# One conv channel tile handed to ScalarE and adding transfers during the attention, and the sum after the convolution placed later, in a two-layer decoder trunk

## The chip, the cores and the metric

The kernel runs on one core of one Trainium2 chip. The metric is the device time of one execution in microseconds. Every other time is from a hardware profile of one execution, measured from the start of its span.

## The reference

It is a trunk of two layers over 512 tokens with 16 learned meta tokens ahead of them (528 positions), 1024 channels, all in float32:

```python
for i in range(2):
    if i == 0: h = h + fox_conformer_mixer(rms_norm(h), ...)      # the change lies here
    else:      h = h + multiscale_pool_mixer(rms_norm(h), ...)
    h = h + conv_glu_ffn(rms_norm(h), ...)                        # 2 x 2816 channels up, 2816 down
return rms_norm(h)[:, 16:]

def fox_conformer_mixer(h, ...):
    q, k, v, f_logit, glu = split(h @ w_in)                       # 3 x 512, 8, 2 x 512 columns
    attn = forgetting_attention(q, k, v, log_sigmoid(f_logit + b_f))   # 8 heads of 64, causal
    a, g = split(glu)
    u = causal_depthwise_conv(a * sigmoid(g), conv_w, conv_b)     # 512 channels, 31 taps
    u = silu(layer_norm(u, ln_g, ln_b))
    return concat([attn, u]) @ w_out
```

## The kernel before, in words

Activations lie transposed: channels on the 128 partitions, the 528 positions along the free axis. The 512 conv channels are four tiles of 128x528. Products run in split float32: an operand becomes a high part (`...H`) and the rest (`...L`), and a product is three matmuls, in two halves of 264 columns. Weights come in chunks of eight 128x128 tiles: SyncE loads `raw` (512 KB), ScalarE writes `wH` and the negated `wL` (L172, L177), and a transfer of POOL's queue adds `raw` onto `wL` (L178). Three buffers of each hold the chunks.

The even mixer takes about the first 265 us. First come the tiles `a` and `g` of the gated input (`GLU_ORDER`); then the attention, whose order on TensorE is written out by hand in the string `PE_ORDER`. `F` is half of a q, k or v tile (24 matmuls), `O` half of an output tile, and a name with a digit is a step of the attention for the head pair of that digit, A and B being its two heads: `MA` (row maxima of the scores; matmuls into `m`, L664 reduces them into `N`, and L666 to L668 make the pair `E` from that), `EA` (transposes `E` into `e`, which goes into `q2`), `SA` (scores `s`; ScalarE exponentiates them twice, L719 and L721, and VectorE takes the low part `PL`, L722), `V` (transposes v; `VH`, `VL`), `A0` and `A1` (scores times values into `o`). `SUM`, `MEAN`, `VAR` and `SILU` are the layer norm of the convolution.

The convolution runs on VectorE meanwhile. As soon as a gated tile `u[i]` is there, its 31 taps go into the list `queue`. `fill(pace)` is called after each unit of the input products and takes the next `pace` taps off the list. Tap 0 of a tile is a scaled copy with bias on ScalarE (L498); each of the other 30 is one multiply-add on VectorE in place (L500). `PACE` holds the pace by stage: 1.8 while the GLU products run, 2.8 in the first part of the attention, then 5.8. `ln_sum` (`SUM`) empties the list, frees the buffers of `u` and of the even head pairs, adds up the four conv tiles (L762, L772) and loads the residual `hm`; `ln_mean` (`MEAN`) is the matmul `mu` over that sum and what follows it.

Only TensorE's order is fixed by hand there (`manual_schedule`). The queues of the others are ordered by a planner before the run: it goes through the instructions in the order in which they were issued and puts into an engine's queue what its own timeline says is ready, so a tap can stand ahead of work issued before it. At run time each engine works off its queue in order. `after(late, early)` is an edge for the planner alone, without a wait. `COPIES` says for each head pair which engine makes the five kinds of rounded copies of q, k and v (A is ScalarE, V is VectorE).

Of the kernel before, what the change touches and what calls it, by code (L numbers as in the profile page):

```python
# [7 lines left out]
F32 = mybir.dt.float32  # L8
F32R = mybir.dt.float32r
BF16 = mybir.dt.bfloat16  # L10
AF = mybir.ActivationFunctionType
ALU = mybir.AluOpType
# [3 lines left out]
P = 128  # L16
T = 528
# [44 lines left out]
PE_ORDER = ("F F F F F F MA0 F MB0 F EA0 F SA0 V0 EB0 F A10 SB0 / "  # L62
# [3 lines left out]


OUTER = (0, 4)
# [15 lines left out]
POOL_ORDER = ("Z0 S0 D0 Z1 X0 S1 D1 Z2 S2 T2 D2 Z3 S3 Q0 X1 T3 D3 Z4 S4 Q1 X2 T4 D4 Z5 S5 Q2 X3 T5 D5 "  # L84
              "Z6 S6 Q3 X4 T6 D6 Z7 S7 Q4 X5 T7 D7 Q5 X6 X7 Q6 Q7")

PACE = (1.8, 2.8, 5.8, 5.8, 5.8, 5.8)

APART = (2,0,1,0)
SPLIT_FIRST = True  # L90
SQ_AFTER = (None, 0, None, None, 4, None, 6, 7)
NORM_AT = 1

COPIES = ('AAAAA', 'VAAAV', 'AAAAA', 'AAVAV')

FIRST_CHUNKS = 3

# [26 lines left out]
def trunk_kernel(  # L124
# [7 lines left out]
    nc = tc.nc  # L132
# [5 lines left out]
    wk = ctx.enter_context(tc.tile_pool(name="wk", bufs=2))  # L138
# [11 lines left out]
    state = {"pos": 0, "emitted": 0}  # L150
# [6 lines left out]
    def col(c, rows=slice(0, P)):  # L157
        return pt[rows, c:c + 1]
# [52 lines left out]
    cell = {}  # L211
# [14 lines left out]
    def after(late, early):  # L226

        tc.add_manual_dep(late.ins, early.ins.name,
                          mybir.DependencyInfo(mybir.DependencyClass.NoSync, mybir.DependencyReason.DATA),
                          reason="order")  # L230
# [75 lines left out]
    with ExitStack() as mx:  # L306
        mp = mx.enter_context(tc.tile_pool(name="mix", bufs=1))
# [46 lines left out]


        cv = h[0:4]
        scr = h[4:8]
        cH = [mp.tile([P, T], F32R, tag=f"cH{i}", name=f"cH{i}") for i in range(NCONV)]
        aH = [mp.tile([P, T], F32R, tag=f"aH{i}", name=f"aH{i}") for i in range(4)]
# [61 lines left out]
        H8 = slice(0, HEADS)  # L421
# [51 lines left out]
        def done_g(i):  # L473
            t_ = wk.tile([P, T], F32, tag="sq", name=f"sg{i}", bufs=3)

            def fn(hf, ps):
                nc.vector.tensor_tensor(t_[:, half(hf)], ps, cell["R"][:, half(hf)], op=ALU.mult)
                i_ = nc.scalar.activation(t_[:, half(hf)], t_[:, half(hf)], AF.Sigmoid)
                after(i_, state["lastexp"])
                if i == NCONV - 1 and hf == 1:  # L480
                    state["set"] = use_log_exp(i_)
                if hf == 1:
                    uu = u[i][:, CW - 1:]
                    nc.vector.tensor_tensor(uu, uu, t_, op=ALU.mult)
                    for j in range(CW):
                        queue.append((i, j))
            return fn

        def cw(i, j):
            return col(C_CW + i * CW + j)  # L490

        queue = []
        credit = [0]

        def tap(i, j):
            src = u[i][:, j:j + T]
            if j == 0:
                nc.scalar.activation(cv[i], src, AF.Identity, scale=cw(i, j), bias=col(C_CB + i))  # L498
            else:
                nc.vector.scalar_tensor_tensor(cv[i], src, cw(i, j), cv[i], op0=ALU.mult, op1=ALU.add)  # L500

        def fill(pace):
            credit[0] = min(credit[0] + pace, len(queue))
            while credit[0] >= 1:
                tap(*queue.pop(0))
                credit[0] -= 1


        def first_products():

            cell["f"] = wk.tile([P, T], F32, tag="tapp", name="f")[H8, :]
            low = wk.tile([P, T], F32, tag="tapp", name="flow")[H8, :]
            pss = [sp(f"zf{hf}")[0:40, :TH] for hf in range(2)]
            a0 = [pp(f"ps_a0_{hf}")[:, :TH] for hf in range(2)]
            ws = [next_weight(("in", "a", 0, k)) for k in range(KT)]
            sums = [sp(f"ssq{x}")[:, :TH] for x in range(2)]
            for k in range(KT):
                sq = first_square(k)
                for x in (xH, xL):
                    for hf in range(2):  # L520
                        mm(pss[hf], wfs[:, k, :], x[k][:, half(hf)], k == 0 and x is xH, k == KT - 1 and x is xL)
                    for hf in range(2):
                        mm(a0[hf], ws[k][0], x[k][:, half(hf)], k == 0 and x is xH, False)
                square_sums(sums, 0, [sq], k == 0, k == KT - 1)
            for hf in range(2):
                for k in range(KT):
                    mm(a0[hf], ws[k][1], xH[k][:, half(hf)], False, k == KT - 1)
                pending.append((done_a(0), hf, a0[hf]))
            for hf, ps in enumerate(pss):
                nc.scalar.copy(cell["f"][:, half(hf)], ps[H8, :])  # L530
                nc.scalar.copy(low[:, half(hf)], ps[32:40, :])
            nc.vector.tensor_tensor(cell["f"], cell["f"], low, op=ALU.add)
            return sums
# [71 lines left out]
        def attention(p):  # L605
# [25 lines left out]
            def maxima(hh):  # L631
                tl = st[hh]
                N = tl["N"]
                for x, parts in enumerate((((2, 0, 272), (1, 0, 144), (0, 0, 16)), ((3, 0, 400),),
                                           ((4, 0, TH),), ((4, TH, T),))):
                    s_ = sp(f"m{p}_{hh}_{x}")
# [28 lines left out]
                E = tl["E"]  # L665
                nc.vector.tensor_tensor(N[:, 4:5], N[:, 4:5], N[:, 5:6], op=ALU.min)  # L666
                nc.vector.tensor_copy(E[:, :, 0], N[:, 0:5])
                nc.vector.tensor_tensor(E[:, :, 1], N[:, 0:5], E[:, :, 0].bitcast(F32), op=ALU.subtract)  # L668

            def rows(hh):  # L670
                tl = st[hh]
# [88 lines left out]
        def sum_of(x, y, name):  # L760
            t_ = wk.tile([P, T], F32, tag="sq", name=name, bufs=3)
            nc.vector.tensor_tensor(t_, x, y, op=ALU.add)  # L762
            return t_

        def ln_sum():
            fill(len(queue))
            early.close()
            lp = mx.enter_context(tc.tile_pool(name="late", bufs=1))
            cL.extend(lp.tile([P, T], F32R, tag=f"cL{i}", name=f"cL{i}") for i in range(NCONV))
            hm.extend(lp.tile([P, T], F32, tag=f"hm{m}", name=f"hm{m}") for m in range(KT))  # L770
            a1, a2 = sum_of(cv[0], cv[1], "mu0"), sum_of(cv[2], cv[3], "mu1")
            nc.vector.tensor_tensor(a1, a1, a2, op=ALU.add)  # L772
            cell["mu"] = a1
            for m in range(KT):
                nc.sync.dma_start(hm[m], hT[:, m, :])

        def ln_mean():
            pss = channel_mean(cell["mu"], "mu")
            for i in range(NCONV):
                for hf in range(2):  # L780
                    nc.vector.scalar_tensor_tensor(cv[i][:, half(hf)], pss[hf], -1.0 / (P * NCONV),
                                                   cv[i][:, half(hf)], op0=ALU.mult, op1=ALU.add)
            for i in range(NCONV):
                s_ = wk.tile([P, T], F32, tag="tapp", name=f"csq{i}")
                nc.scalar.activation(s_, cv[i], AF.Square)
                if i == 0:
                    first = s_
                elif i == 1:
                    cell["var"] = sum_of(first, s_, "var")
                else:  # L790
                    nc.vector.tensor_tensor(cell["var"], cell["var"], s_, op=ALU.add)
# [410 lines left out]
```

## Time and profile before

| | |
|---|---|
| time, median of 3 runs | 1074.52 us (1073.5 to 1074.99) |
| the profiled execution | 1075.98 us, of which the span is 1074.2 us |
| TensorE, matmul | 96% of the span busy |
| ScalarE | 58% |
| VectorE | 51% |
| GpSimd (POOL) | 17% |
| granted TensorE clock, mean | 0.981 of 2.4 GHz |

Busy shares are means over stages that differ much. The views below give, for a stretch, the busy time of each engine (with the number of instructions), the granted clock and the mean share of the 16 DMA engines; for a wait, who waited for whom; and for a DMA, how long it took from its issue to its landing.

### The profile page before, as it was taken

To read this page: it belongs to the slowest core of one execution; us is meant where nothing else is said; L and a number is where in the kernel's file an instruction comes from. 1 tells how busy PE (TensorE), PEld (TensorE's weight loads), DVE (VectorE), ACT (ScalarE), POOL (GpSimd) and SP (SyncE) were. 2 spreads that over 40 slices of the span, in tenths; PEclk is the share of its full clock that TensorE was granted. 3 is DMA by queue.
4 is the path that set the end of the run, shared out by engine and by line. 5 is a ranking of instruction groups with operands and counts; after the bars stand their busy time and mean duration, and the time that the engine had idled before them with its cause. 6 is when DMAs were issued, how large, how long until landed. Compare 5 with 4: busy or idle time off the path is not lost.

```text
span 1074.2 us, 20092 instructions
## 1 busy us (share of the span) xinstructions
PE 1033.4 (96%) x8376; PEld 1021.7 (95%) x8376; DVE 548.9 (51%) x917; ACT 623.7 (58%) x876; POOL 181.4 (17%) x302
## 2 busy tenths in 40 slices
PE   9996879999999999999999998799999999999996
PEld 8996879999999999999999998699999999999995
DVE  5799996876048641035444225608742125445214
ACT  7662647786467653345556557457764345565542
POOL 5210111001111111111111112311111111111111
PEclk9998889999999999999999999799999999999998
DMA  6774223637978778778777777977888788787852
GB/s 218 170 189 114 55 65 85 194 77 173 254 165 181 180 178 200 166 182 180 176 187 179 175 186 169 196 175 181 179 195 191 168 189 178 187 189 185 190 117 79
DMA packets 53291, 179.85 MB, mean 167 GB/s; under 512 B 6352, under 2 KB 8400, under 8 KB 53200
## 3 DMA queue, kind: packets, MB, share of 16 engines
q0 software_dynamic: 25136, 86.65, 44.7%
q1 hardware_dynamic: 26720, 90.68, 25.8%
q8 instruction: 66, 1.08, 0.4%
q10 hardware_dynamic: 1344, 1.23, 0.4%
q14 instruction: 25, 0.20, 0.1%
HBM read 89.80 MB, written 2.10 MB: 86 GB/s over the span
## 4 chain that ended last, share of the span: by engine, by line
PE 82%; DVE 12%; ACT 2%; issue 2%; DMA 1%; POOL 0%; DVEq 0%; POOLq 0%; ACTq 0%
PE up L197 47%; PE dn L197 23%; DVE h L500 7%; PE wo L197 3%; PE ps_v L197 1%; DMA h<-ws 1%; PE ps_k L197 1%; PE ps_q L197 1%; PE pl L197 1%; PE s L197 1%; PE o L197 1%; PE ssq L197 1%; PE m L197 1%; DVE N L664 1%; DVE PL L722 0%
## 5 line engine op out<-in xcount | busy, mean ns | idle before, releaser
L172 ACT CAST wH<-raw 128x1024 fp32r<-128x1024 f32 x162 | 170.0, 1049 | 252.3 <-PE up L197 122.0
L197 PE MATMUL up<-xH,wH 128*128 128x264 f32 (+1 forms) x1408 | 287.3, 286 | 8.1 <-ACT xH L261 8.0
L197 PE MATMUL up<-xL,wH 128*128 128x264 f32 (+1 forms) x1408 | 287.5, 286 | 1.2 <-DVE xL L262 1.2
L197 PE MATMUL up<-xH,wL 128*128 128x264 f32 (+1 forms) x1408 | 286.9, 285 | 0.0
L178 POOL DMA_DIRECT2D wL<-raw x159 | 136.9, 861 | 796.7 <-ACT wL L177 744.8
L197 PEld LDWEIGHTS up<-xH,wH 128*128 128x128 f32 x1408 | 220.5, 190 | 9.3 <-ACT xH L261 9.3
L197 PEld LDWEIGHTS up<-xL,wH 128*128 128x128 f32 x1408 | 220.0, 190 | 2.6 <-DVE xL L262 2.6
L197 PEld LDWEIGHTS up<-xH,wL 128*128 128x128 f32 x1408 | 219.5, 190 | 0.0
L177 ACT ACTIVATE wL<-wH 128x1024 fp32r<-128x1024 f32 x159 | 167.3, 1052 | 1.9
L928 DVE SCALAR_TENSOR_TENSOR t<-u,par,t 128x528 f32<-128x528 f32 (+1 forms) x176 | 131.0, 759 | 57.9 <-ACT t L925 54.8
L197 PE MATMUL dn<-gH,wH 128*128 128x264 f32 (+1 forms) x704 | 145.5, 282 | 0.0
L197 PE MATMUL dn<-gH,wL 128*128 128x264 f32 (+1 forms) x704 | 145.2, 282 | 0.0
L197 PE MATMUL dn<-gL,wH 128*128 128x264 f32 (+1 forms) x704 | 145.2, 281 | 0.0
L197 PEld LDWEIGHTS dn<-gH,wH 128*128 128x128 f32 x704 | 110.2, 188 | 0.1
L197 PEld LDWEIGHTS dn<-gL,wH 128*128 128x128 f32 x704 | 110.0, 188 | 0.1
L197 PEld LDWEIGHTS dn<-gH,wL 128*128 128x128 f32 x704 | 109.7, 188 | 0.0
L979 DVE TENSOR_TENSOR h<-dn,h 128x528 f32<-128x528 f32 (+1 forms) x30 | 21.0, 700 | 173.5 <-PE dn L197 173.5
L958 DVE TENSOR_TENSOR u<-up,R 128x528 f32<-128x528 f32 (+1 forms) x74 | 51.7, 701 | 103.9 <-PE up L197 103.6
L500 DVE SCALAR_TENSOR_TENSOR h<-u,par,h 128x528 f32<-128x528 f32 x120 | 86.1, 755 | 0.3
L925 ACT ACTIVATE t<-u,par 128x528 f32<-128x528 f32 (+1 forms) x88 | 71.0, 820 | 0.0
L214 ACT CAST gH<-t 128x528 fp32r<-128x528 f32 (+1 forms) x44 | 27.5, 624 | 44.2 <-DVE t L939 44.0
L215 DVE TENSOR_TENSOR gL<-t,gH 128x528 fp32r<-128x528 f32 (+1 forms) x44 | 30.8, 700 | 25.8 <-ACT gH L214 25.6
(246 smaller groups left out, 1423.5 us busy)
## 6 DMA issues: line engine op xcount, KB each, us to landing
raw<-wts SPq DMA_DIRECT2D x162, 512.0 KB, 4.5
wL<-raw POOLq DMA_DIRECT2D x159, 512.0 KB, 6.2
h<-hT SPq DMA_DIRECT2D x8, 264.0 KB, 5.4
hm<-hT SPq DMA_DIRECT2D x8, 264.0 KB, 4.9
acc<-sq POOLq DMA_DIRECT2D x7, 264.0 KB, 3.3
h<-ws POOLq DMA_DIRECT2D x5, 264.0 KB, 7.6
outT<-y ACTq DMA_DIRECT2D x1, 512.0 KB, 3.1
outT<-y SPq DMA_DIRECT2D x1, 512.0 KB, 3.9
```

Source lines behind the costliest of these rows:

```text
L172: nc.scalar.copy(wH, raw)
L177: nc.scalar.mul(wL, wH.bitcast(F32), -1.0)
L178: nc.gpsimd.dma_start(wL, raw, accum_op=ALU.add)
L197: nc.tensor.matmul(out, lhsT, rhs, start=start, stop=stop)
L214: nc.scalar.copy(oH, src)
L215: nc.vector.tensor_tensor(oL, src, oH.bitcast(F32), op=ALU.subtract)
L500: nc.vector.scalar_tensor_tensor(cv[i], src, cw(i, j), cv[i], op0=ALU.mult, op1=ALU.add)
L664: nc.vector.tensor_reduce(n_, so, axis=AX.X, op=ALU.max, negate=True)
L925: nc.scalar.activation(t_, uu[:, off + 2:off + 2 + nt], AF.Identity, scale=col(c0 + 2), bias=col(c0 + 3))
L928: nc.vector.scalar_tensor_tensor(t_, uu[:, off + x:off + x + nt], col(c0 + x), t_, op0=ALU.mult, op1=ALU.add)
L958: nc.vector.tensor_tensor(v2(ud), ps[:, :, :nu], v2(R[:, tu:tu + 2 * nu]), op=ALU.mult)
L979: nc.vector.tensor_tensor(v2(h[m][:, td:]), ps[:, :, :nd], v2(h[m][:, td:]), op=ALU.add)
```

## The change

- `ADDED = 3`: the taps of conv tile 3 go into a list of their own with its own pace. Tap 0 stays. Tap 1 is a scaled copy on ScalarE into a new tile `cv2`. Each of taps 2 to 30 is a scaled copy on ScalarE into one of three `tapp` buffers, and a transfer of POOL's queue that adds the buffer onto `cv[3]` (even taps) or `cv2` (odd taps).
- `PACE` is a pair for each stage: VectorE's taps 1.8, 2.2, then 3.2; the new list's 0, 0, then 2.1.
- A tap on VectorE gets an edge for the planner behind the last `E` (L668) issued before it, once there is one.
- `SUM` stands behind the last `F`, seven places later in `PE_ORDER`; `MEAN` comes one `EA3` and one `O` later, and `VAR` one `O` later.
- `ln_sum` adds `cv2` onto `cv[3]` on VectorE first.
- All rounded copies go to ScalarE. `tapp` has three buffers in place of two.

```diff
-            "/ V2 F EA2 F SA2 EB2 F A02 SUM A12 SB2 F B02 MA3 B12 F MEAN EA3 O O MB3 O SA3 O V3 VAR O EB3 O SB3 A03 A13 O SILU O O O O O B03 B13 O O O O")
+            "/ V2 F EA2 F SA2 EB2 F A02 A12 SB2 F B02 MA3 B12 F SUM EA3 O MEAN O MB3 O SA3 O V3 O VAR EB3 O SB3 A03 A13 O SILU O O O O O B03 B13 O O O O")
-PACE = (1.8, 2.8, 5.8, 5.8, 5.8, 5.8)
+ADDED = 3
+PACE = ((1.8, 0.0), (2.2, 0.0), (3.2, 2.1), (3.2, 2.1), (3.2, 2.1), (3.2, 2.1))
-COPIES = ('AAAAA', 'VAAAV', 'AAAAA', 'AAVAV')
+COPIES = ('AAAAA', 'AAAAA', 'AAAAA', 'AAAAA')
+        cv2 = mp.tile([P, T], F32, tag="cv2", name="cv2")
-                        queue.append((i, j))
+                        queue[int(i == ADDED)].append((i, j))
-        queue = []
-        credit = [0]
-        def tap(i, j):
+        queue = {0: [], 1: []}
+        credit = [0, 0]
+        def tap(i, j, kind):
             src = u[i][:, j:j + T]
             if j == 0:
                 nc.scalar.activation(cv[i], src, AF.Identity, scale=cw(i, j), bias=col(C_CB + i))
+            elif kind == 1 and j == 1:
+                nc.scalar.activation(cv2, src, AF.Copy, scale=cw(i, j))
+            elif kind == 0:
+                i_ = nc.vector.scalar_tensor_tensor(cv[i], src, cw(i, j), cv[i], op0=ALU.mult, op1=ALU.add)
+                if "rows" in state:
+                    after(i_, state["rows"])
             else:
-                nc.vector.scalar_tensor_tensor(cv[i], src, cw(i, j), cv[i], op0=ALU.mult, op1=ALU.add)
+                pr = wk.tile([P, T], F32, tag="tapp", name=f"tap{i}_{j}", bufs=3)
+                nc.scalar.activation(pr, src, AF.Copy, scale=cw(i, j))
+                nc.gpsimd.dma_start((cv[i], cv2)[j % 2], pr, accum_op=ALU.add)
         def fill(pace):
-            credit[0] = min(credit[0] + pace, len(queue))
-            while credit[0] >= 1:
-                tap(*queue.pop(0))
-                credit[0] -= 1
+            for kind in range(2):
+                credit[kind] = min(credit[kind] + pace[kind], len(queue[kind]))
+                while credit[kind] >= 1:
+                    tap(*queue[kind].pop(0), kind)
+                    credit[kind] -= 1
-                nc.vector.tensor_tensor(E[:, :, 1], N[:, 0:5], E[:, :, 0].bitcast(F32), op=ALU.subtract)
+                state["rows"] = nc.vector.tensor_tensor(E[:, :, 1], N[:, 0:5], E[:, :, 0].bitcast(F32), op=ALU.subtract)
         def ln_sum():
-            fill(len(queue))
+            fill((len(queue[0]), len(queue[1])))
+            nc.vector.tensor_tensor(cv[ADDED], cv[ADDED], cv2, op=ALU.add)
```

## Rows read from the trace of the kernel before

**Rows 1.** The chain that ended last, by engine, over the whole span.

```profile
PE 82%; DVE 12%; ACT 2%; issue 2%; DMA 1%; POOL 0%; DVEq 0%; POOLq 0%; ACTq 0%
```

**Rows 2.** Busy time by stage; the last three numbers: clock, DMA share, GB/s.

```profile
40.00:83.00 43.00, 41.82 (x345) 41.44 (x343) 42.87 (x72) 26.98 (x35) 9.95 (x15) 1.00 0.79 183
83.00:161.00 78.00, 60.63 (x446) 57.54 (x447) 77.12 (x154) 35.19 (x78) 9.21 (x15) 0.87 0.31 75
161.00:204.00 43.00, 43.00 (x362) 41.59 (x360) 28.60 (x73) 31.11 (x73) 4.70 (x7) 1.00 0.54 145
```

**Rows 3.** Waits of TensorE, 81 to 162 us: sum, times, longest.

```profile
PE e L197 <- DVE E L668: 8.2, 1, 8.2
PE e L197 <- DVE N L666: 5.6, 1, 5.6
PE o L197 <- DVE PL L722: 2.8, 2, 1.6
PE m L197 <- DVE k L590: 0.9, 1, 0.9
PE o L197 <- DVE VL L622: 0.6, 1, 0.6
```

**Rows 4.** Timeline of VectorE around two makings of E: start, busy time.

```profile
92.87 0.14 DVE L666 TENSOR_TENSOR N<-N 128x1 f32<-128x1 f32 x1
...
94.10 2.78 DVE L500 SCALAR_TENSOR_TENSOR h<-u,par,h 128x528 f32<-128x528 f32 x4
...
100.92 0.17 DVE L668 TENSOR_TENSOR E<-N,E 128x5 fp32r<-128x5 f32 x1
...
170.74 0.16 DVE L666 TENSOR_TENSOR N<-N 128x1 f32<-128x1 f32 x1
170.94 0.17 DVE L667 CAST E<-N 128x5 fp32r<-128x5 f32 x1
171.14 0.17 DVE L668 TENSOR_TENSOR E<-N,E 128x5 fp32r<-128x5 f32 x1
```

**Rows 5.** Busy time by stretch, of ps_q, ps_k and s alone (TensorE first).

```profile
143.00:150.00 7.00, 5.51 (x24) 5.38 (x24) 0.43 (x1) 0.56 0.01 2
170.00:174.00 4.00, 3.16 (x24) 2.99 (x24) 0.33 (x1) 1.00 0.60 115
...
101.00:107.00 6.00, 4.54 (x24) 4.43 (x24) 0.00 (x0) 0.68 0.20 79
...
118.00:122.00 4.00, 3.43 (x17) 3.16 (x14) 1.79 (x6) 0.52 0.53 162
183.00:186.00 3.00, 1.95 (x17) 1.81 (x14) 0.44 (x2) 1.00 0.00 0
```

**Rows 6.** Busy time by stretch, of the taps on VectorE (L500) alone.

```profile
40.00:83.00 43.00, 34.80 (x50) 1.00 0.79 183
83.00:161.00 78.00, 50.48 (x70) 0.87 0.31 75
```

**Rows 7.** Timelines of VectorE, and the chain that ended last, near the sum.

```profile
67.61 0.69 DVE L484 TENSOR_TENSOR u<-u,sg 128x528 f32<-128x528 f32 x1
...
136.81 0.70 DVE L762 TENSOR_TENSOR mu<-h,h 128x528 f32<-128x528 f32 x1
...
162.64 0.69 DVE L772 TENSOR_TENSOR mu<-mu,mu 128x528 f32<-128x528 f32 x1
...
203.44 0.89 PE mu L197 x4
```

**Rows 8.** One line of ScalarE: nanoseconds least, median, most.

```profile
L261 ACT ACTIVATE xH<-h,par x30: 720/722/737, 4.4 to 696.2; 128x528 fp32r<-128x528 f32 x30
```

**Rows 9.** The page's DMA issues: count, size, median us from issue to landing.

```profile
acc<-sq POOLq DMA_DIRECT2D x7, 264.0 KB, 3.3
h<-ws POOLq DMA_DIRECT2D x5, 264.0 KB, 7.6
```

**Rows 10.** Timeline of POOL in the pooling layer; brackets: idle before, and its releaser.

```profile
684.11 0.85 POOL L249 DMA_DIRECT2D acc<-sq  x1 [1.88 <-ACT wL L177]
...
688.00 0.85 POOL L249 DMA_DIRECT2D acc<-sq  x1 [1.28 <-DMA acc<-sq]
```

More of the change, by code (lines that the diff above doesn't have):

```diff
@@ L498, in tap @@
                 nc.scalar.activation(cv[i], src, AF.Identity, scale=cw(i, j), bias=col(C_CB + i))
-            else:
-                nc.vector.scalar_tensor_tensor(cv[i], src, cw(i, j), cv[i], op0=ALU.mult, op1=ALU.add)
+            elif kind == 1 and j == 1:
[4 more added lines that the diff above has]
+                    after(i_, state["rows"])
+            else:
+                pr = wk.tile([P, T], F32, tag="tapp", name=f"tap{i}_{j}", bufs=3)
+                nc.scalar.activation(pr, src, AF.Copy, scale=cw(i, j))
+                nc.gpsimd.dma_start((cv[i], cv2)[j % 2], pr, accum_op=ALU.add)
         def fill(pace):
-            credit[0] = min(credit[0] + pace, len(queue))
-            while credit[0] >= 1:
-                tap(*queue.pop(0))
-                credit[0] -= 1
+            for kind in range(2):
[3 more added lines that the diff above has]
+                    credit[kind] -= 1
         def first_products():
-            cell["f"] = wk.tile([P, T], F32, tag="tapp", name="f")[H8, :]
-            low = wk.tile([P, T], F32, tag="tapp", name="flow")[H8, :]
+            cell["f"] = wk.tile([P, T], F32, tag="tapp", name="f", bufs=3)[H8, :]
+            low = wk.tile([P, T], F32, tag="tapp", name="flow", bufs=3)[H8, :]
             pss = [sp(f"zf{hf}")[0:40, :TH] for hf in range(2)]
@@ L783, in ln_mean @@
             for i in range(NCONV):
-                s_ = wk.tile([P, T], F32, tag="tapp", name=f"csq{i}")
+                s_ = wk.tile([P, T], F32, tag="tapp", name=f"csq{i}", bufs=3)
                 nc.scalar.activation(s_, cv[i], AF.Square)
```

## The prediction, on record before the changed kernel ran

> **What bounds the kernel now.** I read the chain that ended last first: 82% TensorE and 12% VectorE [rows 1]. So most of the kernel is matmuls back to back, and one stretch is not. The table of stages shows which [rows 2]: from 83 to 161 us VectorE is busy 77.1 of 78 us while TensorE has 60.6, and its clock is 0.87 in the mean; from 161 to 204 us TensorE is busy without a gap at full clock and VectorE only 28.6 of 43. The reader is to see a bound that changes hands at 161 us, where the taps end.
>
> The waits of TensorE in the first of these stretches sum to 18.1 us, all on VectorE [rows 3]. Two of them, 8.2 and 5.6 us, are for `E`, the pair made from the row maxima. The timeline of VectorE shows why [rows 4]: from L666 at 92.87 to the end of L668 at 101.09 is 8.2 us where the same three instructions without taps take 0.6 us (170.74 to 171.31). Groups of four taps (2.78 us) stand in the queue between one and the next. The waits cost a second time: after them TensorE runs near 1.2 GHz for a while, at a granted clock of 0.56, 0.68 and 0.52 over the stretches shown. The same 24 matmuls take 5.51 and 4.54 us in place of 3.16, the 17 of `s` 3.43 in place of 1.95 [rows 5]: 2.35 + 1.38 + 1.48 = 5.2 us. So 18.1 + 5.2 = 23.3 us is all that this stage has to give.
>
> **The change part by part.** *The edge behind `E`, and the lower pace.* A tap issued after a `MA` may no longer stand ahead of that `MA`'s `E`. By the paces, 23 taps are issued while the GLU products run (13 calls at 1.8) and 13 in the six F ahead of `MA0`, 36 of the 93; two of them are tap 0 on ScalarE. Only older taps can then delay `E`, and 34 taps of 0.70 us (34.80/50, [rows 6]), 24 us, are done well before 83 us, since the kernel before had done 50 by then. So `E` of the first `MA0` comes about 1 us after its reductions, and one F (about 3 us) lies between `MB0` and `EA0`. I take back both long waits and the slow clock behind them: 8.2 + 5.6 + 1.38 + 2.35 = 17.5 us, and the 0.9 us for `k`, whose cause is also taps in front. The three short waits in `A10` (2.8 + 0.6, and 1.48 of clock, 4.9 us) I keep: the 13 or so taps issued between `MB0` and `MA1` all become free just there, and ScalarE gets more to do ahead of `PL`. Bounds for this part: 0 (other waits take their place) and 23.3. Taken: 18.4.
>
> *What VectorE has left.* It loses the 30 taps of tile 3. But the edge leaves it idle before 83 us, where it was busy 42.9 of 43 us [rows 2]. After 83 us it has 93 - 3 - 34 = 56 taps of 0.72 us (50.48/70, [rows 6]), 40.4 us; the rest of its work to 204 us stays, 77.1 + 28.6 - 50.5 = 55.2 us, and the added sum is 0.7 us by the like adds [rows 7]. That makes 96 us, while TensorE at its floor needs 121 - 23.3 = 98 us for the same steps. The rounded copies that leave VectorE (three pairs or groups, an estimate of under 3 us) give it a little air. So VectorE is booked nearly full to the end, and what it owes last is the sum: behind `E` of `MA3` come 3 taps of the last F and 3 that the paces leave over, 6 x 0.72 = 4.3 us, then `cv2` onto `cv[3]` and two adds of 0.7, in all 0.6 + 4.3 + 2.1 = 7.0 us and the attention's own work in between (one or two us), against about 6 us of TensorE from `MA3` to `MEAN` (an F of 3.16, the values, `EA3` and an O). TensorE waits there. The sum was ready 40 us early before (162.64 + 0.69 against 203.44, [rows 7]), so this cost is new. Bounds: 0, and 9 us if only nine tenths of VectorE's time can be used (96/0.9 - 98). Taken: 3.0.
>
> *ScalarE.* 30 copies with a scale at 0.72 us each, the row of the same form [rows 8], are 21.6 us, and the moved rounded copies an estimate of 3 us more. Its load from 83 to 204 was 35.2 + 31.1 = 66.3 us of 121; it becomes 91 of 98 if none of the products is made earlier, and some are, since tile 3 is complete at 68.3 us [rows 7]. It had the room, but each product can stand 0.7 us in front of an exponential or a rounded copy that TensorE waits for. Nothing, if all lie in its gaps; for the other end see the rivals. Taken: 2.0.
>
> *The transfers.* 29 of 264 KB, each 0.85 us of POOL [rows 10], 24.7 us on a queue that was busy 9.2 + 4.7 = 13.9 us from 83 to 204. Two sums by turns keep two in flight, as a transfer must wait for the last one on its own sum. Where one sum waited so, the next went out 3.9 us after it (684.11 to 688.00, landing 3.3, [rows 9, 10]): 1.95 us a transfer with two, 57 us in all. With the landing of the slower row, 7.6 + 0.6 = 8.2 us a pair, 4.1 a transfer, 119 us. The share of the DMA engines is 0.31 in this stage [rows 2], so nearer to the first; I take 3.0, 87 us. They can start at 68.3: the planner does not hold work to the place of its issue, as the add at 136.81, issued with `SUM`, shows [rows 7]. So they end near 155 us, ahead of `SUM` near 178, and cost nothing on the path. What covers them is these 23 us; if it goes, `MEAN` is late. Behind a waiting transfer on POOL stand the weights' `wL` transfers, and behind those SyncE's loads of `raw`, two chunks ahead of TensorE.
>
> The Trainium skill, "DMA: Bandwidth & Descriptors", section "Anatomy of one DMA — SWDGE (gpsimd) path", gives about 2.0 us plus the bytes at 436 GB/s, 2.6 us for such a transfer as an estimate; the row of 3.3 lies above that and the row of 7.6 far above, so the rows are used. By the page the chain would take 29 x (2.6 + 0.6)/2 = 46 us and the sum below would be the same.
>
> *Edits costed at nothing.* `SUM`, `MEAN` and `VAR` later: the same matmuls in another order, with as many O between `MEAN` and `VAR` as before. The loads of `hm` on SyncE's queue wait, as before, for buffers that `SB2` frees; two F and `MA3` cover them. `tapp`'s third buffer only removes waits.
>
> **The sum.** 18.4 - 3.0 - 2.0 = 13.4 us, 1075.98 - 13.4 = 1062.6 for a profiled execution. That execution stands 1.5 us above the median of the runs, so 1061 us. What follows `MEAN` is bound by TensorE and moves up with it.
>
> **The rivals.**
>
> *All of it comes back.* `A10` stops waiting and the sum is in time: 1075.98 - 23.3 - 1.5 = 1051 us. For it: the waits of rows 3 are all VectorE's. Against: 96 us of work for 98.
>
> *VectorE is still the bound.* If the edges leave it idle at the wrong times, so that it works only four fifths of the time, it needs 120 us after 83 for its 96 and `MEAN` stands where it stood: 1074 us; at 0.85 it needs 113 us, 1067. For it: the idle it now has ahead of 83 us, and the taps bunched behind each `E`. Against: from 161 to 204 us, two thirds booked, it made TensorE wait for nothing.
>
> *The other side: ScalarE waits for the buffers.* A product needs its `tapp` free, so its transfer three before must have landed, and ScalarE's queue is in order: exponentials, weights and copies stand behind a product that waits. The planner sets products as early as its own idea of a landing allows; each landing later than that is a wait on ScalarE. Such a wait on POOL was 1.28 us [rows 10]. 26 products wait: 33 us, less the 7 us that ScalarE has free, 26 us against a gain of 13.4: 1061 + 26 = 1087 us. It decides from (13.4 + 7)/26, 0.8 us a product. For it: the landings of rows 9 differ by more than twice. Against: ScalarE's load leaves gaps, and TensorE has an F between most steps.
>
> *The adds set the end.* If the transfers only start with their place of issue, in the second part of the attention near 104 us, and take 4.1 us each, they end at 223, the adds at 225, and `MEAN` moves from 203 to 225: 1095 us. At the same start it decides from 3.4 us a transfer. For it: the paces hold the list to that place. Against: the add at 136.81.
>
> **How the numbers follow.** Changes within 0.2% (2.1 us) can't be told from none. Chances: the forecast 0.52, 1055 to 1068; all of it 0.13; VectorE still bound 0.12 (faster 0.06, same 0.04, slower 0.02); ScalarE waiting 0.17 (0.02 faster, 0.02 same, 0.13 slower); the adds 0.06, slower. Faster 0.73, same 0.06, slower 0.21. The range from 1051 to 1082 leaves out half of the second case, the adds and the worse half of ScalarE's: about 0.2.
>
> **What the profile after would show.** Right: no wait of TensorE for `E` over 1 us, no taps between L666 and L668, the clock at 1.00 from 83 us on, `mu` on TensorE near 190, the last adding transfer landed before the last taps. Wrong: ScalarE idle ahead of products with a DMA as the releaser, POOL idle ahead of adding transfers while a `wL` is due, TensorE waiting for `s`'s exponentials or for weights, or `MEAN` waiting for a transfer and not for VectorE.

## The result, and the profile after

The changed kernel takes 1084.66 us in the median of 4 runs (1080.49 to 1086.39); the kernel before, beside it, 1074.21 us (1073.5 to 1074.99). The ratio is 1.0082 with a 95% interval of 1.0067 to 1.0097: slower by 0.8%, where 1061 us was forecast and 1082 us was the end of the range. The profiled execution took 1086.39 us, its span 1084.6 us.

To see where it went I split each span at two instructions of TensorE: the first product of q (end of the gated input) and the first `up` (start of the feed-forward layer). Between them lies the attention, the convolution and their output product, in short the mixer. Before: 63.61 us to its start, 201.83 us of mixer, 808.8 us after it. After: 65.66, 209.48 and 809.5 us. Of the 10.4 us that the span grew, 7.65 are the mixer, 2.05 lie in front of it, where none of the changed work runs, and 0.7 behind it. The forecast was a mixer 13.4 us shorter.

The same stages as [rows 2], of the changed kernel; the columns are busy time (and count) of TensorE, its weight load, VectorE, ScalarE and GpSimd, then clock, DMA share and GB/s:

```profile
40.00:83.00 43.00, 43.00 (x358) 43.00 (x356) 34.93 (x56) 26.38 (x36) 13.54 (x19) 1.00 0.82 188
83.00:161.00 78.00, 58.69 (x433) 55.34 (x432) 50.70 (x108) 55.79 (x109) 32.54 (x41) 0.86 0.90 180
161.00:204.00 43.00, 42.20 (x345) 40.51 (x345) 38.81 (x85) 31.40 (x74) 4.11 (x6) 0.98 0.37 87
```

From 83 to 161 us VectorE has fallen from 77.1 to 50.7 us of work, as intended, and TensorE does no more than before: 58.7 us. The DMA share has gone from 0.31 to 0.90. None of the engines is full, so the stage is bound by waits. The largest of TensorE's, 60 to 270 us (sum, times, longest; [rows 3] are the ones of before):

```profile
PE tv L629 <- ACT P L735: 8.5, 1, 8.5
PE o L199 <- DVE h L756: 4.1, 2, 3.5
PE mu L199 <- DVE mu L787: 3.5, 1, 3.5
PE o L199 <- DVE PL L736: 2.0, 1, 2.0
PE s L199 <- DVE VL L635: 1.9, 1, 1.9
PE m L199 <- ACT k L225: 1.4, 1, 1.4
```

The two waits for `E` are gone, and TensorE waits for no weight. The largest wait is now one for ScalarE's exponentials `P`, and ScalarE, VectorE and GpSimd wait for something that none of them waited for here before, the landing of a tap's adding transfer (60 to 215 us):

```profile
POOL h L512 <- DMA h<-tap: 18.5, 6, 5.4
POOL cv L512 <- DMA cv<-tap: 14.8, 8, 4.4
ACT tap L510 <- DMA h<-tap: 13.3, 10, 4.0
ACT tap L510 <- DMA cv<-tap: 9.8, 9, 1.5
DVE h L785 <- DMA h<-tap: 1.6, 1, 1.6
```

The timeline of ScalarE ahead of the longest wait of TensorE shows how the one becomes the other (start, busy time; in brackets the idle time before it and its releaser):

```profile
95.05 0.74 ACT L510 ACTIVATE tap<-u,par 128x528 f32<-128x528 f32 x1 [2.05 <-DMA h<-tap]
97.28 0.74 ACT L510 ACTIVATE tap<-u,par 128x528 f32<-128x528 f32 x1 [1.50 <-DMA cv<-tap]
...
103.62 0.74 ACT L510 ACTIVATE tap<-u,par 128x528 f32<-128x528 f32 x1 [4.00 <-DMA h<-tap]
104.26 2.32 ACT L225 CAST q<-h 64x528 fp32r<-64x528 f32 x4
106.60 1.06 ACT L179 ACTIVATE wL<-wH 128x1024 fp32r<-128x1024 f32 x1
107.56 1.35 ACT L510 ACTIVATE tap<-u,par 128x528 f32<-128x528 f32 x2
108.82 0.47 ACT L733 ACTIVATE PH<-s 128x384 fp32r<-128x384 f32 x1
109.19 0.48 ACT L735 ACTIVATE P<-s 128x384 f32<-128x384 f32 x1
```

TensorE had finished the scores at 101.26 us; `tv` takes a buffer of the scores' kind, and so waits for exponentials. These stood in ScalarE's queue behind a product whose buffer was not free before 103.62, a landing, and behind what had piled up: copies of q, a weight, two more products. They begin at 108.82, and `tv` at 109.72. The clock makes it dearer: the next 24 matmuls, of `ps_k`, take 4.84 us at a granted clock of 0.60 (mean of 108 to 117 us), against 3.16 for 24 such matmuls at full clock [rows 5].

### The profile page after: what moved, and what is told of

Read it like the earlier page. It is cut to its first block, busy times and chain, and to the rows that moved or that the text cites. A ratio compares the mean times of both kernels' runs of the same rounds, so it can differ in the third digit from the quotient of the medians.

```text
span 1084.6 us, 20140 instructions
## 1 busy us (share of the span) xinstructions
PE 1037.1 (96%) x8376; PEld 1024.2 (94%) x8376; DVE 530.9 (49%) x880; ACT 647.2 (60%) x914; POOL 207.2 (19%) x331
## 4 chain that ended last, share of the span: by engine, by line
PE 79%; DMA 7%; issue 5%; ACT 4%; DVE 3%; POOL 1%; DVEq 0%; SPq 0%; POOLq 0%; ACTq 0%
PE up L199 46%; PE dn L199 23%; DMA h<-tap 3%; PE wo L199 3%; DMA cv<-tap 1%; DMA h<-ws 1%; PE ps_k L199 1%; PE pl L199 1%; PE ssq L199 1%; PE ps_v L199 1%; DVE h L505 1%; PE ps_q L199 1%; DMA h<-hT 1%; DMA hm<-hT 1%; PE o L199 0%
## 5 line engine op out<-in xcount | busy, mean ns | idle before, releaser
L505 DVE SCALAR_TENSOR_TENSOR h<-u,par,h 128x528 f32<-128x528 f32 x90 | 67.8, 762 | 1.2
```

The lines of the kernel that those rows point to most:

```text
L505: i_ = nc.vector.scalar_tensor_tensor(cv[i], src, cw(i, j), cv[i], op0=ALU.mult, op1=ALU.add)
```

## The experiments

Profiles of one kernel are compared by the three stretches; the times are medians of runs made beside runs of the kernel before. All numbers first:

| run | us | ratio, 95% interval | to q | mixer | behind it |
|---|---|---|---|---|---|
| before | 1074.21 | | 63.61 | 201.83 | 808.8 |
| after | 1084.66 | 1.0082 [1.0067, 1.0097] | 65.66 | 209.48 | 809.5 |
| e1 no transfers | 1070.95 | 0.9955 [0.9937, 0.9972] | 64.51 | 196.03 | 809.0 |
| e2 all taps on VectorE | 1071.18 | 0.9966 [0.9947, 0.9984] | 64.02 | 197.12 | 808.0 |
| e5 places alone | 1073.21 | 0.9987 [0.9975, 0.9999] | 64.01 | 204.11 | 803.3 |
| e13 copies as before | 1083.51 | 1.0086 [1.0072, 1.0099] | 63.67 | 214.06 | 803.6 |
| e12 small transfers | 1075.98 | 1.0014 [1.0003, 1.0025] | 64.00 | 199.90 | 809.8 |
| e3 products don't wait | 1081.76 | 1.0055 [1.0037, 1.0073] | 65.61 | 211.37 | 803.1 |
| e4 products held | 1075.29 | 1.0004 [0.9990, 1.0018] | 64.02 | 206.28 | 803.1 |
| e16 final add held | 1077.41 | 1.0028 [1.0015, 1.0041] | 64.03 | 206.93 | 804.5 |
| e15 and three sums | 1074.21 | 1.0001 [0.9986, 1.0015] | 64.28 | 203.45 | 804.3 |
| e14 and no product waits | 1074.13 | 0.9998 [0.9985, 1.0011] | 65.63 | 202.24 | 803.3 |
| e9 adds on GpSimd | 1088.53 | 1.0126 [1.0112, 1.0140] | 65.65 | 214.15 | 807.8 |
| e6 E edge, two pairs | 1064.55 | 0.9902 [0.9888, 0.9915] | 63.99 | 194.74 | 803.2 |
| e10 E edge, three pairs | 1071.39 | 0.9971 [0.9961, 0.9982] | 65.66 | 196.14 | 807.9 |
| e7 eight transfers | 1065.72 | 0.9913 [0.9901, 0.9926] | 64.03 | 195.37 | 805.3 |
| e11 eight, three pairs | 1065.87 | 0.9913 [0.9900, 0.9927] | 64.02 | 195.95 | 806.1 |
| e8 eight, two pairs | 1058.80 | 0.9862 [0.9841, 0.9884] | 63.99 | 184.04 | 808.5 |

The last column matters for the reading. Behind the mixer all kernels do the same work, yet it takes 803 to 810 us, whatever the mixer took. The traces place the difference. All kernels agree within 0.6 us from the first `up` to the start of the second feed-forward layer, 400 us later, and again from that layer's `ssq` to the end; in between lie 51 to 57 us in which TensorE waits for `xH` (8.0 us before, 5.4 us in e5). The last of these waits goes with the time behind the mixer. At 422 to 428 us behind the first `up` ScalarE waits for the landing of an adding transfer of the pooling layer, 2.9 to 4.4 us in the nine kernels with 806 us or more and at most 2.1 us in the others; from 425 to 460 us the granted clock is 0.90 to 0.95 in the former and 1.00 in the latter. The changed kernel (809.5 us) and e4 (803.1):

```profile
702.51 0.73 ACT L263 ACTIVATE xH<-h,par 128x528 fp32r<-128x528 f32 x1 [4.38 <-DMA h<-ws]
```

```profile
693.54 0.74 ACT L263 ACTIVATE xH<-h,par 128x528 fp32r<-128x528 f32 x1 [1.72 <-DMA h<-ws]
```

Why that landing is late in some kernels is not shown. So a cause inside the mixer is read from its own column, and a difference of times below some 6 us is not put down to it alone. Each column is of one profile, so a difference of one or two us in it is not put down to an edit either.

### One part alone

**e1**: the products stay on ScalarE, their transfers are left out, and with them most of tile 3's convolution.

```diff
-                nc.gpsimd.dma_start((cv[i], cv2)[j % 2], pr, accum_op=ALU.add)
```

> Leaves out the 29 adding transfers (the conv of tile 3 is then incomplete); the products on ScalarE stay, each into its buffer. Theory A (ScalarE's queue stands in order behind products that wait for a buffer, because the transfers land late): ScalarE's 23 us of waits for DMAs go, TensorE's wait of 8.5 us at V0 goes with them, and the time falls to 1060 to 1068 us. Theory B (ScalarE's and VectorE's added load and the late sum are enough): ScalarE keeps its 21.6 us of products, so the time stays above 1078 us.

Measured: 13.6 us less than the changed kernel by the ratios (1.27%), and the mixer 13.45 us shorter; 1070.95 us lies between the two ranges that I had named, nearer to theory A's. So the term that I had put at nothing is the largest. TensorE's waits from 60 to 270 us sum to 13.5 us in place of 24.3, which is 10.8 of the 13.45. The largest that are left:

```profile
PE o L199 <- ACT P L737: 3.7, 2, 2.9
PE mu L199 <- DVE mu L786: 3.5, 1, 3.5
PE tv L628 <- ACT P L734: 3.2, 1, 3.2
```

With the products alone TensorE still waits 3.7 + 3.2 = 6.9 us for `P`; without products (e2, below) it is 2.4 us.

**e2**: no handover at all; the 124 taps of all four tiles on the list of VectorE (120 of them multiply-adds there), at its old paces. **e5**: the kernel before with the new places of `SUM`, `MEAN` and `VAR`. **e13**: the changed kernel with the rounded copies on their old engines.

```diff
e2:
-                        queue[int(i == ADDED)].append((i, j))
+                        queue[0].append((i, j))
e13:
-COPIES = ('AAAAA', 'AAAAA', 'AAAAA', 'AAAAA')
+COPIES = ('AAAAA', 'VAAAV', 'AAAAA', 'AAVAV')
```

> All four conv tiles on VectorE at the old pace (2.8, then 5.8), no products on ScalarE, no transfers; the edge behind E, the later sum and the copies on ScalarE stay. Tells what the edge is worth by itself. If the order of VectorE's queue was the whole cost before, the 13.8 us of waits for E and the slow clock behind them go, 1058 to 1064 us. If VectorE's amount of work is the bound, 81 taps of 0.72 us and 55 us of other work after 83 us need 113 us or more in place of 96, the sum is late and the time is 1070 to 1080 us.

> The kernel before with only the new places of SUM, MEAN and VAR. The sum was ready 40 us early there, so if the places alone cost nothing the time is 1073 to 1076 us. If the later MEAN pushes the layer norm's chain onto the last output tiles, up to 1.15 us more for each O it passes: 1076 to 1078 us.

> The changed kernel with the PSUM copies' engines as in the kernel before (q, k and the values' copies back where they were). Theory (the copies moved to ScalarE are worth little either way): within 3 us of the changed kernel, 1082 to 1087 us. Rival (ScalarE, which holds the products and waits for landings, is what the copies wait behind): 1076 to 1081 us.

Measured: with the places alone the mixer is 2.3 us longer, while the time is in the range for places that cost nothing. The copies at their old places change the time by 0.04%, as the theory had it, and the mixer by +4.6 us, so moving them was not what cost. e2's 1071.18 us lies in the range of the second theory, that VectorE's amount of work is the bound. Its waits for `E` are down to 3.5 us and the mixer is 4.7 us shorter, but `mu` waits 8.1 us: ten taps run one after the other between `E` of the last `MA` ahead of the sum and the sum. A wait is taken from the front and part of it handed on to the end.

### What it is about the transfers

**e12**: each transfer moves 16 of 528 columns. **e3**: the transfers read `u` in place of the product, so that no product waits for its buffer; the sum is not the convolution. **e4**: the products get the planner's edge behind `E`, too.

```diff
e12:
-                nc.gpsimd.dma_start((cv[i], cv2)[j % 2], pr, accum_op=ALU.add)
+                nc.gpsimd.dma_start((cv[i], cv2)[j % 2][:, :16], pr[:, :16], accum_op=ALU.add)
e3:
+                nc.gpsimd.dma_start((cv[i], cv2)[j % 2], src, accum_op=ALU.add)
e4:
+                i_ = nc.scalar.activation(pr, src, AF.Copy, scale=cw(i, j))
+                after(i_, state["rows"])
```

> The changed kernel, but each of its 29 adding transfers moves 16 of the 528 columns, so most of the convolution's adds are left out; products, order of issue and waits stay. Theory (the loss is the landing time of large transfers, for which the engines' in-order queues wait): landings fall below 3 us, the waits for them on ScalarE and GpSimd shrink to a third or less, and the time is 1068 to 1074 us, as without transfers. Rival (it is the waits and the order itself, whatever the size): over 1078 us.

> The transfers read the gated tile itself in place of the product's buffer (the conv of tile 3 is then unscaled), so that products and transfers both stay in number and size but no product waits for a landing. Theory A, with the waits on ScalarE as the cause: its 23 us of DMA waits go and the time falls to 1063 to 1070 us, though POOL still waits for landings and the DMA engines are as full. Theory C (the traffic itself: full DMA engines, late weights, POOL's queue in order): the time stays above 1078 us and TensorE waits for weights.

> Each product of the transfers also gets the edge behind the last E issued before it, so the first transfers start in the attention, when the DMA engines are less full, and none is ahead of its place. Theory A with the early crowding as its cause: landings of 264 KB fall from 4.6 to 4.9 us to under 4, the wait at V0 goes, and the time is 1066 to 1074 us. If any wait on a landing in ScalarE's queue costs as much wherever it is, or if the last transfers now come late for the sum, it stays at 1080 to 1090 us with the loss moved to later steps or to the matmul of the sum.

The page's DMA issues give count, size and median us from issue to landing, first of the changed kernel:

```profile
h<-tap POOLq DMA_DIRECT2D x15, 264.0 KB, 4.6
cv<-tap POOLq DMA_DIRECT2D x14, 264.0 KB, 4.9
```

and of e12:

```profile
h<-tap POOLq DMA_DIRECT2D x15, 8.0 KB, 2.7
cv<-tap POOLq DMA_DIRECT2D x14, 8.0 KB, 3.4
```

Small transfers still take more than half of the time to land. ScalarE's waits for them fall from 23.1 to 7.3 us and the mixer by 9.6 of the 13.45 us; 3.9 us stay. The time, 1075.98 us, lies between what the theory and the rival expected. The transfers' size is most of the cost; what is left, small transfers' waits and their issuing on GpSimd, is not separated further.

e3 took 23 us of waits off ScalarE and the mixer became 1.9 us longer. That refutes theory A, by which ScalarE's queue alone is the cause; the time is where theory C put it, though weights are the smaller part of TensorE's waits. The waits of e3, TensorE's and then the others':

```profile
PE e L199 <- DVE h L756: 12.9, 1, 12.9
PE ps_q L199 <- DMA wL<-raw: 4.5, 1, 4.5
```

```profile
POOL h L512 <- DMA h<-u: 22.3, 12, 4.4
DVE h L785 <- DMA h<-u: 15.8, 1, 15.8
POOL cv L512 <- DMA cv<-u: 14.0, 10, 3.7
```

The planner now believed in an earlier chain and put the final add of the two sums (L785) early into VectorE's queue, where it stood 15.8 us; the weights' `wL` stood behind waiting transfers on GpSimd's. In e4, too, the wait moved: `tv` waits 0.7 us and ScalarE 7.5, but the chain starts at 84.59 us, 12.8 us later, VectorE's final add waits 7.0 us for it and `mu` 9.6. The landings stay at 4.5 us. The mixer is 3.2 us shorter, and the time, 1075.29 us, lies between the two ranges named.

**e16**: the changed kernel with the final add held behind the last `E`. **e15**: three sums by turns in place of two, and the final adds held. **e14**: e15, and the transfers read `u` (the sum is not the convolution), so that no product waits.

```diff
e16:
+            i_ = nc.vector.tensor_tensor(cv[ADDED], cv[ADDED], cv2, op=ALU.add)
+            after(i_, state["rows"])
e15:
+        cv2 = [mp.tile([P, T], F32, tag=f"cv2{x}", name=f"cv2{x}") for x in range(2)]
...
+                nc.gpsimd.dma_start((cv[i], *cv2)[j % 3], pr, accum_op=ALU.add)
```

> The changed kernel, two sums, with the final add held until the edge rows of the last pair emitted before it. Theory (three sums leave each transfer's predecessor more time to land, and that gave back the 10 us): this edit alone changes nothing beyond 2 us, 1082 to 1087 us. Rival (the early place of the final add in VectorE's queue cost it): 1074 to 1078 us.

> The same three sums and held final adds, with the true products as the transfers' source: a full version of the change. Theory (products wait for the landings that free their three buffers, whatever the number of sums): ScalarE still waits 10 us or more for landings and the time is 1077 to 1084 us. Rival (it was the order of two sums that spaced the landings out): under 4 us of waits on ScalarE and 1070 to 1075 us.

> The changed kernel with three sums by turns instead of two (28 transfers), the transfers read a slice of u instead of the product (so the convolution's values are not the reference's, and no product waits for a landing), and the final adds held until the edge rows of the last pair. Theory (the loss is in-order queues that wait for landings): waits for landings on ScalarE are gone, on VectorE under 2 us, on GpSimd under 10 us, and the time is 1069 to 1075 us, as without transfers (1070.95). Rival (the transfers' traffic itself costs, through late weights): ScalarE waits for nothing of theirs and the time is still 1078 to 1084 us, with waits for weights on TensorE.

e16's time is 0.54% below the changed kernel's, in the rival's range and against my theory that this edit does nothing. But in its mixer it is only 2.55 us; the start (1.6 us) and the part behind the mixer (4.9 us), where the edit does nothing, make up the rest of the profile's 9.1 us. Nor is the add shown to cost the 2.55 us. In the changed kernel VectorE waits at it, from 152.63 to 154.27 us:

```profile
151.86 0.77 DVE L505 SCALAR_TENSOR_TENSOR h<-u,par,h 128x528 f32<-128x528 f32 x1
154.27 0.71 DVE L785 TENSOR_TENSOR h<-h,cv 128x528 f32<-128x528 f32 x1 [1.64 <-DMA h<-tap]
```

The 24 matmuls of `ps_k` near 152 us do take longer than in e16. Busy time of `ps_k` alone from 149 to 158 us (TensorE, its weight load, VectorE; clock, DMA share, GB/s), changed kernel and then e16:

```profile
149.00:158.00 9.00, 4.71 (x24) 4.53 (x24) 0.43 (x1) 0.81 0.73 130
```

```profile
149.00:158.00 9.00, 3.16 (x24) 2.97 (x24) 0.85 (x2) 1.00 0.68 147
```

But they run at the lower clock from their first, 0.12 us into VectorE's wait, and wait for nothing themselves:

```profile
152.75 0.52 PE L199 MATMUL ps_k<-xH,wH 128*128 128x264 f32 x1
153.06 0.42 PE L199 MATMUL ps_k<-xL,wH 128*128 128x264 f32 x1
```

In e16 the first two take 0.37 and 0.28 us. So these 1.55 us of the 2.55 are not the add's. What TensorE did before is two waits, 1.01 us at 145.0 and 1.86 us at 151.6; in e16 it is the second alone, 1.75 us. What may be the add's is a wait for `PL` behind it, 2.02 us against 1.22.

With three sums (e15) a transfer waits for the one three before it. The waits for landings fall from 23.1 to 15.6 us on ScalarE and from 33.3 to 6.5 on GpSimd; the last transfer is issued at 140.83 instead of 150.85 us, and the mixer is 3.5 us shorter than e16's; the wait of `tv` has gone from 9.0 to 5.6 us. ScalarE's waits are those of the theory, the time is the rival's. It is a full version of the change that ties with the kernel before. e14, without any wait of ScalarE for a tap's landing, is no faster: the products no longer held the transfers back, and `ps_q` waited for the low part of a weight that stood behind them on GpSimd:

```profile
PE ps_q L199 <- DMA wL<-raw: 7.2, 1, 7.2
```

The time came out as the theory of in-order queues said, 1069 to 1075 us, but by luck: GpSimd waits 28.7 us for landings, where the theory had under 10.

**e9**: the adds on GpSimd itself, no transfers.

```diff
-                nc.gpsimd.dma_start((cv[i], cv2)[j % 2], pr, accum_op=ALU.add)
+                nc.gpsimd.tensor_tensor(to, to, pr, op=ALU.add)
```

> The changed kernel with each of the 29 adding transfers replaced by an add on GpSimd itself (128x528, near 1.8 us by the 0.91 us of the 128x256 products at the end), so the same sum without a landing. If late landings and full DMA engines are what the change pays for, ScalarE's waits fall under 5 us and the time is 1066 to 1073 us. If GpSimd's adds slow VectorE where both read two operands, the taps take longer than 0.77 us each and the time stays above 1078 us with the sum later than before.

1088.53 us, as the second theory had it: ScalarE's waits for landings are gone, and VectorE is slowed instead (last section).

### Fewer transfers, and the edge where it pays

**e6** and **e10** are e2 with the edge for the first two or three pairs alone. **e7** hands over ten taps of tile 3 and not 30: two scaled copies into two new sums, eight products and eight transfers. **e11** and **e8** are e7 with the edge for three and two pairs.

```diff
e6 (e10: p < 3):
+                if p < 2:
+                    state["rows"] = i_
+                else:
+                    state.pop("rows", None)
e7:
+PACE = ((1.8, 0.0), (2.6, 0.0), (4.6, 2.1), (4.6, 2.1), (4.6, 2.1), (4.6, 2.1))
+                        queue[int(i == ADDED and 1 <= j <= 10)].append((i, j))
+                nc.gpsimd.dma_start(cv2[j % 2], pr, accum_op=ALU.add)
```

> As the edge alone (all taps on VectorE, no transfers), but the edge holds taps only behind the E of the first two head pairs; from the third pair on a tap may run ahead again. If the 8.1 us that the edge alone made the sum's matmul wait come from the ten taps held behind the last E, that wait falls to 2 to 4 us and the time to 1064 to 1068 us. If VectorE is simply full (its idle time after 83 us was under 9 us), the wait stays near 6 us and new waits for E of the third pair come: 1069 to 1073 us.

> All tap products and sums on VectorE again (no ScalarE products, no adding transfers), the late sum and the moved copies stay, and the taps are held behind E for the first three pairs alone (with two pairs: 1064.55 us, with all four: 1071.18 us). Theory (an E wait of 7.0 us was left at the third pair, and the mean's wait is paid only where taps are held behind E of the last pair): the third pair's E wait goes, the mean waits about 2 us, 1058 to 1063 us. Rival (taps held behind the third pair's E pile up in front of the sum just the same): the mean's wait is 5 us or more and the time 1066 to 1071 us.

> Ten of tile 3's taps leave VectorE in place of 30: two scaled copies straight into two sums, and eight products with eight adding transfers, four to a sum; the other taps stay on VectorE, the pace is 2.6, then 4.6. If the cost goes with the number of transfers whose landing is waited for (13.6 us for 29), it is about 4 us here; VectorE has 7 us less than with the edge alone, so 1066 to 1071 us, and ScalarE's waits for DMAs sum to 5 to 8 us. If any transfer among the weights costs by displacing the order of the queues, not by its number, the time stays above 1075 us.

> Ten taps of one tile leave VectorE (two scaled copies and eight products on ScalarE, eight adding transfers), and the taps are held behind E for the first three pairs alone (with all four pairs: 1065.72 us). Theory (few transfers are free, and the rest of the loss is the taps held behind the last E): the mean's wait falls from 8.8 us to 3 us or less, 1057 to 1062 us, the fastest of all. Rival (ScalarE's extra products take back what VectorE saves): 1063 to 1067 us, no better than without any transfer.

> Eight adding transfers, and the taps held behind E for the first two pairs alone: the two ways that were fastest so far (1065.72 and 1064.55 us) in one. Theory (ten taps less on VectorE are ten taps less in front of the third pair's E): its wait falls from 7.0 to 1 us or less and the time to 1057 to 1061 us. Rival (VectorE's stock decides little by now, as the three-pair runs suggest): 1063 to 1067 us.

e6 comes out at 1064.55 us, in the first range named, with a wait of 7.0 us for `E` left; `mu` waits 1.8 us. The 7.0 us stand in front of `EA3`, so this `E` is the fourth pair's, not the third's as the expectations of e8 and e10 have it:

```profile
PE e L199 <- DVE E L681: 9.3, 2, 7.0
PE mu L199 <- DVE mu L789: 1.8, 1, 1.8
```

e10 takes that wait away and gets it back at the sum:

```profile
PE mu L199 <- DVE mu L789: 8.1, 1, 8.1
PE e L199 <- DVE E L681: 3.5, 2, 2.2
```

It is 11.1 and 11.6 us, and mixers of 194.7 and 196.1: the stock of taps is the same, it only stands in front of one wait or the other. My expectation for e10 was wrong, its rival right in the wait (the time is 0.4 us above its range). These waits are also e2's, and as in e2 ten taps stand behind the last `E`, though e10 does not hold them there:

```profile
189.83 8.00 DVE L504 SCALAR_TENSOR_TENSOR h<-u,par,h 128x528 f32<-128x528 f32 x10
```

So it is not the edge behind the last pair that puts them in front of the sum; between e6 and e10 the edge behind the third makes the difference.

e7 and e11 take ten taps off VectorE but hold the rest behind the third `E`: seven taps still stand between the last `E` and the sum, `mu` waits 8.8 and 8.6 us, and the mixers of 195.4 and 196.0 are little shorter than e2's and e10's. The times are 1065.72, just below the range expected (ScalarE waits 2.1 us for landings, not 5 to 8), and 1065.87, the rival's. e8 takes the same ten taps off and does not hold the rest; the sum is done ahead of the last `E`, and the wait for that `E` is 0.4 us. Neither step is worth much alone (e2 to e6 2.4 us of mixer, e2 to e7 1.75), both together 13.1. In e8 `mu` starts at 187.71 us without a wait, and the largest wait of TensorE in the mixer is for an `E` of the second pair (3.4 us at 129.43):

```profile
PE e L199 <- DVE E L682: 3.8, 2, 3.4
```

ScalarE waits 2.3 us for the landings of its eight transfers, VectorE not at all. The mixer takes 184.04 us, 17.8 less than before, and the time is 1058.80 us, as expected and 0.9862 of the kernel before: the fastest version found.

## Why the prediction was wrong

**The edge behind `E` (18.4 us): right in mechanism.** [rows 4] had four taps between the three instructions that make `E`. After, on VectorE:

```profile
88.23 0.16 DVE L679 TENSOR_TENSOR N<-N 128x1 f32<-128x1 f32 x1
88.43 0.23 DVE L680 CAST E<-N 128x5 fp32r<-128x5 f32 x1
88.69 0.17 DVE L682 TENSOR_TENSOR E<-N,E 128x5 fp32r<-128x5 f32 x1
```

TensorE waits for no `E`. The gain did not come: what it got back was used up by other waits: from 60 to 270 us TensorE waits 24.3 us for other engines, where before it was 19.8 us over the same stretch, the 18.1 of [rows 3] among them.

**The late sum (3.0 us): right in size.** `mu` waits 3.5 us for VectorE, and the six taps booked behind the last `E` do stand there; the final add, booked with them, ran at 154.27. `mu` starts at 213.10 us rather than near 190, because everything ahead of it is late.

**The step that failed: "So they end near 155 us, ahead of `SUM` near 178, and cost nothing on the path."** The first half held: 29 transfers from 71.75 us to the last issue at 150.85 and a landing near 154, 2.84 us each where I took 3.0. The second half did not follow from it. The term asks when the chain ends; who stands in line at each of its links was left to a rival (ScalarE) and to a remark (GpSimd), and has no price in the sum. The transfers cost 13.45 us of mixer (e1), and their landings stop three queues that are worked off in order: products on ScalarE with exponentials behind them, the final add on VectorE with taps and copies behind it, and the next transfers on GpSimd with the weights' `wL` behind them. Taking the wait from one queue moved it to another (e3, e4, e14); smaller transfers took most of it away (e12), and three sums with a held add 6.0 us of it (e15), 3.5 of these the third sum.

The landing I had from [rows 9], and I leaned to the faster row because the share of the DMA engines is 0.31 in this stage. That reason was wrong: where the rows were taken, 672 to 704 us of the kernel before, the share is 0.89, as high as in the changed stage. The landings of after are 4.6 and 4.9 us; that the chain still came out near the 3.0 us a transfer is in part luck. The Trainium skill, "DMA: Bandwidth & Descriptors", section "Anatomy of one DMA — SWDGE (gpsimd) path", would have had 2.6 us as an estimate; the measured landings decide, and they are far above it.

**ScalarE (2.0 us): the mechanism right, the size not.** Without a single transfer of taps the waits for `P` are 6.9 us (e1), 4.9 more than I took, where without products they are 2.4 (e2). That is the largest part of what else is missing that the traces name: the forecast for a change without transfers' cost was a mixer 13.4 us shorter, e1's is 5.8 us shorter. The rest of these 7.6 us is not split.

**The rival that came nearest was "ScalarE waits for the buffers", 1087 us with a chance of 0.17.** It was to decide from 0.8 us a product; the 26 products waited 23.1 us, 0.89 each in the mean. Its mechanism is in the trace, at the longest wait of all, but e3 shows that it is not the whole: without it the same landings stop VectorE and the weights. I had counted ScalarE's gaps as cover, and a gap covers nothing when it lies behind the waiting instruction, as the 4.00 us ahead of 103.62 show. "The adds set the end" did not happen: the chain was done more than 50 us ahead of the sum.

What stays open: why the landing that goes with the time behind the mixer is late in some kernels. The first product of q comes at 65.6 us in five of these kernels and at 63.6 to 64.5 in the others; only these five have a wait of 1.1 us for `xL` near 10.4 us, and why they have it is open too. The 13.45 us are not split further between the three queues than the runs above allow.

## What to carry to other kernels

Before handing work to a chain of transfers, list for every link which engine's queue holds the instruction that waits for its landing and what stands behind that instruction; that the chain ends in time says nothing about it. A stock of filler work that is as large as the slack moves from one wait to the next when it is reordered (e6 and e10), and taking work off the full engine pays only if what is left is not held back to the end (e7 and e8): here ten taps and the edge for two pairs were enough. Thirty taps were tried with the edge for four pairs alone. Judge an edit by its own stretch of the trace when an unrelated stage varies by as much as the edit is worth.

## What the runs showed of the hardware

Adds with two operands on GpSimd slow VectorE down. In e9, 60 to 215 us (busy time and mean ns of one), and then its taps in the changed kernel:

```profile
L505 DVE SCALAR_TENSOR_TENSOR h<-u,par,h 128x528 f32<-128x528 f32 x70 | 58.3, 839 | 1.1
L513 POOL TENSOR_TENSOR h<-h,tap 128x528 f32<-128x528 f32 x15 | 24.4, 1626 | 3.3 <-ACT tap L510 3.1
```

```profile
L505 DVE SCALAR_TENSOR_TENSOR h<-u,par,h 128x528 f32<-128x528 f32 x70 | 53.2, 765 | 1.1
```

The mean hides that a few instructions take all of it. Six taps take 1398 to 1723 ns, each beside an add of GpSimd; the others stay under 773. The one-column minimum on the way to `E`, 158 to 161 ns when GpSimd adds nothing, takes 7.99 us once and 2.55 us once:

```profile
85.95 7.99 DVE L680 TENSOR_TENSOR N<-N 128x1 f32<-128x1 f32 x1
98.92 0.16 DVE L680 TENSOR_TENSOR N<-N 128x1 f32<-128x1 f32 x1
137.54 2.55 DVE L680 TENSOR_TENSOR N<-N 128x1 f32<-128x1 f32 x1
```

The first begins during an add of GpSimd, and it ends at 93.94 us, when five more adds in a row have ended (93.91). The second stands in front of TensorE's longest wait in e9, 8.5 us. The Trainium skill, "SBUF — State Buffer", section "SBUF: two separate sides", says that a VectorE instruction with two SBUF inputs and a GpSimd one that reads SBUF shut each other out for a whole instruction; the trace agrees, and here one VectorE instruction was shut out by six adds in turn.

The adding transfers of the taps took longer to land than the 3.3 us of [rows 9]: 264 KB took 4.6 and 4.9 us with two sums, 5.8 and 6.3 us with three (e15), and 5.0 to 6.0 us where there were only eight (e7, e8, e11); 8 KB took 2.7 and 3.4 us. What stretches them, each other or the weights beside them, is not separated.
